# Order of the sums in a seven-product quad: one subtraction and the steps that put the sums together

## The chip, the cores and the metric

The kernel runs on one core of one Trainium2 chip. The metric is the device time of one execution in microseconds (us), lower is better; for the kernel before it is the median of 3 runs.

## What is computed

One decoder layer for 256 tokens of width 2048 in float32: sliding-window attention (16 query heads, 4 key/value heads) and an HGRN2 recurrence side by side, merged by sigmoid gates, then a SwiGLU feed-forward of inner width 5632 and a gated per-layer embedding. Cut to the products that matter here (`w_in` is [2048, 9728], `w_gate_up` is [2048, 11264]):

```python
y = rms_norm(x, g_mix_pre) @ w_in          # q, k, v, the HGRN2 inputs, two gates
...
merged = sigmoid(gate_a) * branch_a + sigmoid(gate_h) * branch_h
x = x + rms_norm(merged @ w_out, g_mix_post)
g, u = split(rms_norm(x, g_ffn_pre) @ w_gate_up)
x = x + rms_norm((silu(g) * u) @ w_down, g_ffn_post)
```

All weight products are made to float32 accuracy on a faster matmul format: each operand is split into a rounded part and the rest, and a product is three matmuls.

## The kernel before

**Weights.** They come from memory in pieces of 2 x 128 rows by 512 columns (`raw`, 512 KB, a DMA of SP). ScalarE (ACT) copies a piece to the rounded part `wh`, VectorE (DVE) subtracts it from the piece and so makes `wl`; both go either as one instruction of 1024 columns for the two row blocks, or as one of 512 for each. TensorE (PE) then runs, for 128 rows, `wh` with `hi`, `wh` with `lo` and `wl` with `hi`, where `hi` and `lo` are the same split of the activations.

**Quads.** Some pieces are taken in twos: two row blocks of two column blocks make a quad b11, b21, b12, b22, and the quad is multiplied with 7 products instead of 8 (a Strassen-Winograd form). `parts_of_quad` makes the seven right sides: b11, b21, b22 and the sums t1 = b11 - b12, t2 = b22 + t1, t4 = b21 - t2, t3 = b22 - b12. `hi(name, src)` is the copy on ACT, `lo(name, src)` the subtraction on DVE, `total(a, b, op)` a sum on DVE into a tile `t`. It is a generator: at each `yield` the planner may put other work between. `by_quads` (L520) runs the matmuls of a quad in the order b11, b21, t1, t2, b22, t4, t3. The left sides of the sums (`sides`, split into `shi` and `slo`) are made by DVE and ACT elsewhere. There are 59 quads: in three pairs of the gate columns of w_in (`gate_pair`), in two columns of w_out, in ten of the eleven blocks of w_gate_up (`swiglu`) and in w_down.

**Banks.** PSUM has eight banks of 128 x 512. While a group of quads runs, four hold the plain products (`cs`) and four the sums (t1, t2, t3, b11). `drop` puts a bank at the end of the queue `banks`; `acc` (for matmuls of weights) and `misc` (for transposes and the like) take the first of the queue. So the order of the drops decides which bank the next work gets and which instruction it waits for.

**Putting together.** After the last quad of a group `put_together` (L567) copies the bank of b11 (p1, ACT) and makes from it and the other three sums the four addends u2, u4, u3 and again u2 (DVE). Then `total` (L585) adds to each of the four `cs` banks its addend and drops the bank. This goes on in 16 groups.

**Order.** Instructions are issued in the order in which the Python program emits them, each engine in its own row. A planner with a rough clock for each engine keeps a heap of generators; `yield A`, `yield V` and `yield T` come back when that engine is estimated to be done with what was issued, `yield 0.3` after that many us. `pump` runs the generators that are due, `hurry` pulls them forward when a bank or a side is lacking. `prefetch_quads` (L443) makes the coming quads' parts a step at a time. So one moved line can shift rows elsewhere.

In `swiglu` the products of gate and up are combined when the four totals are done (`ev_g`, `ev_u`), and `gated` then transposes the result on PE: 4 matmuls `misc<-ident,u` of 128 x 128 for each half of the tokens.

Of the kernel before, what the change touches and what calls it, by code (L numbers as in the profile page):

```python
# [17 lines left out]
ALU = mybir.AluOpType  # L18
# [110 lines left out]
def block_kernel(ctx: ExitStack, tc: tile.TileContext, I, out: bass.AP):  # L129
# [55 lines left out]
    V = InOrder(nc.vector, 0.07, 0.00105)  # L185
# [50 lines left out]
    def slot(s, shape=(P, NB), dt=F32):  # L236
        i = free_slots.popleft()
        t = slots.tile(list(shape), dt, tag=f"s{i}", name=nm(s))
        owner[id(t)] = i, t
        return t  # L240

    def free(*tiles):
        for t in tiles:
            free_slots.append(owner.pop(id(t))[0])

    def room(n):

        while len(free_slots) < n:
            yield 0.3
# [13 lines left out]
    def drop(ps):  # L263
        banks.append(bank_of.pop(id(ps))[0])
# [10 lines left out]
    def act(o, i, f, **kw):  # L275
        return A.activation(o, i, f, **kw)

    def tt(o, a, b, op):
        return V.tensor_tensor(o, a, b, op)
# [84 lines left out]
    def parts_of_quad():  # L364

        w, k, col, raw, _ = loaded.popleft()
        other = loaded.popleft()[3]
        b11, b21, b12, b22 = raw[:, 0, :], raw[:, 1, :], other[:, 0, :], other[:, 1, :]
        parts = {}

        def hi(name, src):
            parts[name] = slot("wh", dt=F32R)
            act(parts[name], src, AF.Copy)

        def total(a, b, op):
            t = slot("t")
            tt(t, a, b, op)
            return t

        def lo(name, src):  # L380
            h, t = parts[name], slot("wl", dt=F32R)
            tt(t, src, h.bitcast(F32), ALU.subtract)
            parts[name] = h, t

        hi("b11", b11)
        hi("b21", b21)
        yield
        t1 = total(b11, b12, ALU.subtract)
        hi("t1", t1)
        lo("b11", b11)  # L390
        yield
        t2 = total(b22, t1, ALU.add)
        hi("t2", t2)
        t4 = total(b21, t2, ALU.subtract)
        hi("t4", t4)
        yield
        lo("b21", b21)
        load_more()
        t3 = total(b22, b12, ALU.subtract)
        hi("b22", b22)  # L400
        yield
        hi("t3", t3)
        lo("t1", t1)
        lo("b22", b22)
        load_more()
        free(t1)
        yield
        lo("t2", t2)
        lo("t4", t4)
        free(t2, t4)  # L410
        yield
        lo("t3", t3)
        free(t3)
        ready.append(((w, k, col), parts, None))

    def load_more():
        if plan:
            load_pair()
# [3 lines left out]
    def begin():  # L422

        if not loaded or len(making) > 1:
            return
        if loaded[0][4]:
            if len(loaded) > 1 and len(free_slots) >= STEP + SPARE:
                making.append(parts_of_quad())
                next(making[-1])
        elif len(in_pool) <= SPLIT or len(free_slots) >= ROOMY:  # L430
            making.append(parts_of_pair())
            next(making[-1])
# [87 lines left out]
    def by_quads(w, n, order, lhs, sides, cs, sums, us, start=True, stop=True, evac=None):  # L520
# [4 lines left out]
        for i, (q, seven) in enumerate(order):  # L525
# [38 lines left out]
            if last:  # L564
                chain(put_together(sums, us))

    def put_together(sums, us):  # L567

        yield T
        yield from room(4)  # L570
        p1, u2, u3, u4 = (slot("u") for _ in range(4))
        act(p1, sums["b11"], AF.Copy)
        drop(sums["b11"])
        yield A
        tt(u2, sums["t2"], p1, ALU.add)
        drop(sums["t2"])
        tt(u4, sums["t1"], u2, ALU.add)
        yield V
        tt(u3, sums["t3"], u2, ALU.add)
        drop(sums["t3"])  # L580
        tt(u2, sums["t1"], u3, ALU.add)
        drop(sums["t1"])
        us.extend([[p1, u3], [u4, u2]])

    def total(us, n, c, ps):  # L585
# [1127 lines left out]
    for at, (pair, gi) in enumerate(DOWN):  # L1713
        if at % 5 == 0:
            ps, us = [[acc(), acc()] for n in range(2)], []
            sums = {"left": len(SEVEN_DOWN[pair])}
# [138 lines left out]
```

## Time and profile before

| what | value |
|---|---|
| median of 3 runs | 1487.96 us (1487.32 to 1491.14) |
| the profiled execution | 1489.56 us |
| its span, from the first to the last recorded instruction | 1487.5 us |
| TensorE clock granted, mean | 0.997 |
| DVE rows `u<-acc,u`, steps and totals together | 132, mean 684 ns |
| DVE rows `t<-raw,t` (t2 and t4) | 118, mean 687 ns |

The profile shows one execution. PE, DVE, ACT and SP are engines; a row like `acc<-wh,hi` names the output's tile and the inputs'. In a timeline row stand the start in us from the begin of the span, the time from start to end, the engine, the operation with its shapes, and a count of equal neighbours that are drawn together; in square brackets the idle time ahead of it and what ended that. An instruction of DVE or of PE may start before its forerunner's end as shown, so the distance of two starts is the measure of what one costs in a row, and PE's ends are modelled. All of the kernel's instructions are recorded in a helper, so all have the line L181; the tiles tell them apart.

### The profile page before, as it was taken

How to read it: one execution, taken by the hardware profiler on the slowest of the kernel's cores; microseconds unless marked ns; L12 is line 12 of the kernel's file. 1: busy time of each engine (PE TensorE's matmuls, PEld its weight loads, DVE VectorE, ACT ScalarE, POOL GpSimd, SP SyncE). 2: the span in 40 equal slices, each digit the busy share in tenths (PEclk: the TensorE clock that was granted, in tenths of full speed). 3: DMA queues.
4: the chain of work that ended last, by engine and by line, in shares of the span. 5: the costliest groups of instructions: out<-in, count | busy, mean ns of one | idle time of the engine just before them, and what ended most of it. 6: DMA issues, size and time to landing. Idle time of an engine off the chain costs nothing.

```text
span 1487.5 us, 19958 instructions
## 1 busy us (share of the span) xinstructions
PE 1469.5 (99%) x6838; PEld 1216.3 (82%) x6838; DVE 1239.9 (83%) x2043; ACT 888.9 (60%) x1417; POOL 62.9 (4%) x107
## 2 busy tenths in 40 slices
PE   9999999999999999999999999999999999999997
PEld 6888888888887888888888888888888887888885
DVE  6878958755999867977899999999988899997773
ACT  7755655566666645665655666565655666575661
POOL 2100000000000100000000000000000000010000
PEclk9999999999999999999999999999999999999998
DMA  9754544345576856866756676576677678797551
GB/s 342 257 188 155 171 141 128 114 128 170 184 240 227 309 185 201 272 227 199 252 182 219 205 238 213 174 230 206 215 239 268 214 252 270 214 336 260 192 188 56
DMA packets 159557, 314.59 MB, mean 211 GB/s; under 512 B 11072, under 2 KB 11520, under 8 KB 159456
## 3 DMA queue, kind: packets, MB, share of 16 engines
q1 hardware_dynamic: 153024, 293.38, 61.0%
q0 software_dynamic: 6256, 19.88, 3.7%
q8 instruction: 53, 0.87, 0.2%
q14 instruction: 48, 0.39, 0.1%
q10 hardware_dynamic: 176, 0.07, 0.0%
HBM read 298.08 MB, written 15.21 MB: 211 GB/s over the span
## 4 chain that ended last, share of the span: by engine, by line
PE 64%; DVE 4%; issue 2%; DMA 1%; ACT 1%; DVEq 0%; POOLq 0%; POOL 0%; ACTq 0%
PE acc L181 63%; DVE wl L181 2%; PE misc L181 1%; DVE u L181 1%; ACT wh L181 1%; DVE t L181 1%; DMA raw<-in_w_in 1%; DMA raw<-in_w_down 0%; DMA raw<-in_w_gate_up 0%; DVE eg L181 0%; DVE slo L181 0%; DVE lo L181 0%; ACT hi L181 0%; DVE sides L181 0%; DVE s L181 0%
## 5 line engine op out<-in xcount | busy, mean ns | idle before, releaser
L181 PE MATMUL acc<-wh,hi 128*128 128x512 f32 x1769 | 700.2, 396 | 3.6 <-DVE u L181 2.4
L181 DVE TENSOR_TENSOR wl<-raw,wh 128x1024 fp32r<-128x1024 f32 (+1 forms) x606 | 595.7, 1007 | 115.4 <-ACT wh L181 113.8
L181 PE MATMUL acc<-wl,hi 128*128 128x512 f32 x1769 | 690.0, 390 | 0.0
L181 PE MATMUL acc<-wh,lo 128*128 128x512 f32 x1769 | 688.9, 389 | 0.0
L181 ACT ACTIVATE wh<-raw 128x1024 fp32r<-128x1024 f32 (+1 forms) x606 | 514.3, 883 | 239.8 <-PE acc L181 101.6
L181 PEld LDWEIGHTS acc<-wl,hi 128*128 128x128 f32 x1769 | 332.0, 188 | 71.2 <-DVE wl L181 1.1
L181 PEld LDWEIGHTS acc<-wh,hi 128*128 128x128 f32 x1769 | 332.3, 188 | 70.6 <-DVE u L181 3.2
L181 PEld LDWEIGHTS acc<-wh,lo 128*128 128x128 f32 x1769 | 332.5, 188 | 66.6 <-issue 0.2
L181 ACT ACTIVATE wh<-t 128x512 fp32r<-128x512 f32 x236 | 145.6, 628 | 106.6 <-DVE t L181 85.9
L181 DVE TENSOR_TENSOR wl<-t,wh 128x512 fp32r<-128x512 f32 x236 | 152.2, 683 | 0.5 <-PE acc L181 0.5
L181 DVE TENSOR_TENSOR u<-acc,u 128x512 f32<-128x512 f32 x132 | 86.3, 684 | 18.8 <-PE acc L181 17.6
L181 PE MATMUL acc<-wh,shi 128*128 128x512 f32 x236 | 91.9, 390 | 1.2 <-ACT shi L181 1.2
L181 PE MATMUL acc<-wh,slo 128*128 128x512 f32 x236 | 91.9, 390 | 0.2 <-DVE slo L181 0.2
L181 PE MATMUL acc<-wl,shi 128*128 128x512 f32 x236 | 91.8, 389 | 0.0
L181 DVE TENSOR_TENSOR t<-raw,t 128x512 f32<-128x512 f32 x118 | 81.1, 687 | 3.7
L181 PEld LDWEIGHTS acc<-wh,shi 128*128 128x128 f32 x236 | 44.3, 188 | 10.8 <-ACT shi L181 1.6
L181 PEld LDWEIGHTS acc<-wh,slo 128*128 128x128 f32 x236 | 44.3, 188 | 9.7 <-DVE slo L181 0.5
L181 PEld LDWEIGHTS acc<-wl,shi 128*128 128x128 f32 x236 | 44.3, 188 | 9.2
L181 POOL DMA_DIRECT2D act<-actd x40 | 21.4, 538 | 601.9 <-DVE wl L181 402.4
L181 DVE TENSOR_TENSOR t<-raw,raw 128x512 f32<-128x512 f32 x59 | 40.3, 684 | 3.9 <-DMA raw<-in_w_gate_up 1.9
L181 DVE TENSOR_TENSOR t<-raw 128x512 f32<-128x512 f32 x59 | 40.3, 684 | 0.0
L181 DVE TENSOR_TENSOR lo<-act,hi 128x512 fp32r<-128x512 f32 x40 | 27.2, 684 | 8.1 <-ACT hi L181 8.0
(214 smaller groups left out, 852.1 us busy)
## 6 DMA issues: line engine op xcount, KB each, us to landing
raw<-in_w_gate_up SPq DMA_DIRECT2D x176, 512.0 KB, 4.6
raw<-in_w_in SPq DMA_DIRECT2D x152, 512.0 KB, 4.3
raw<-in_w_down SPq DMA_DIRECT2D x88, 512.0 KB, 5.5
raw<-in_w_out SPq DMA_DIRECT2D x32, 512.0 KB, 5.5
raw<-in_w_ple_gate SPq DMA_DIRECT2D x32, 512.0 KB, 5.1
act<-actd POOLq DMA_DIRECT2D x40, 256.0 KB, 5.6
raw<-in_w_attn_branch SPq DMA_DIRECT2D x16, 512.0 KB, 5.2
raw<-in_w_hgrn_branch SPq DMA_DIRECT2D x16, 512.0 KB, 5.1
```

The source lines that it names most:

```text
L181: return tc.keep_in_program_order(f(o, *a, **kw))
```

## The change

In the quad, the `wl` of b21 is emitted between t2 and t4, and the generator's pause stands before t4. In `put_together` the second value of u2 is t3 + u4 in place of t1 + u3: both are t1 + t2 + t3 + p1. With it the bank of t1 is dropped after the second step and that of t3 after the last, and the pause by V between u4 and u3 becomes two pauses of 0.5 us.

```diff
--- before.py
+++ after.py
@@ -391,10 +391,10 @@
         yield
         t2 = total(b22, t1, ALU.add)
         hi("t2", t2)
+        lo("b21", b21)
+        yield
         t4 = total(b21, t2, ALU.subtract)
         hi("t4", t4)
-        yield
-        lo("b21", b21)
         load_more()
         t3 = total(b22, b12, ALU.subtract)
         hi("b22", b22)
@@ -574,12 +574,13 @@
         yield A
         tt(u2, sums["t2"], p1, ALU.add)
         drop(sums["t2"])
+        yield 0.5
         tt(u4, sums["t1"], u2, ALU.add)
-        yield V
+        drop(sums["t1"])
         tt(u3, sums["t3"], u2, ALU.add)
+        yield 0.5
+        tt(u2, sums["t3"], u4, ALU.add)
         drop(sums["t3"])
-        tt(u2, sums["t1"], u3, ALU.add)
-        drop(sums["t1"])
         us.extend([[p1, u3], [u4, u2]])
 
     def total(us, n, c, ps):
```

No engine gets other work by it, but two instructions of ACT and two of DVE, where a piece of 1024 columns is done in two of 512. The order changes as follows.

**DVE, from the second pair of gate columns to the third.** The group's steps and totals, before: `acc_3985`, `3984`, `3981`, `3980` are its plain banks, `t_4343`, `t_4360`, `t_4364`, `t_4378` the sums t1, t2, t4, t3 of a quad of the next pair.

```order
L181 TENSOR_TENSOR u_4351<-acc_4032,u_4350 128x512
L181 TENSOR_TENSOR u_4350<-acc_4030,u_4351 128x512
L181 TENSOR_TENSOR wl_4410<-t_4360,wh_4362 128x512
L181 TENSOR_TENSOR wl_4412<-t_4364,wh_4366 128x512
L181 TENSOR_TENSOR wl_4414<-t_4378,wh_4388 128x512
L181 TENSOR_TENSOR wl_4338<-raw_4304,wh_4337 128x1024
L181 TENSOR_TENSOR u_4350<-acc_3985,u_4350 128x512
L181 TENSOR_TENSOR u_4352<-acc_3984,u_4352 128x512
L181 TENSOR_TENSOR u_4351<-acc_3981,u_4351 128x512
L181 TENSOR_TENSOR u_4349<-acc_3980,u_4349 128x512
L181 TENSOR_TENSOR wl_4417<-raw_4322,wh_4416 128x1024
```

The same place in the change; t4 is `t_4372` here. Both extracts begin at the group's u3 and the second u2.

```order
L181 TENSOR_TENSOR u_4351<-acc_4032,u_4350 128x512
L181 TENSOR_TENSOR u_4350<-acc_4032,u_4352 128x512
L181 TENSOR_TENSOR wl_4404<-t_4343,wh_4345 128x512
L181 TENSOR_TENSOR wl_4406<-raw_4280,wh_4380 128x512
L181 TENSOR_TENSOR wl_4410<-t_4360,wh_4362 128x512
L181 TENSOR_TENSOR wl_4412<-t_4372,wh_4374 128x512
L181 TENSOR_TENSOR wl_4414<-t_4378,wh_4402 128x512
L181 TENSOR_TENSOR u_4350<-acc_3985,u_4350 128x512
L181 TENSOR_TENSOR u_4352<-acc_3984,u_4352 128x512
L181 TENSOR_TENSOR u_4351<-acc_3983,u_4351 128x512
L181 TENSOR_TENSOR u_4349<-acc_3982,u_4349 128x512
L181 TENSOR_TENSOR wl_4338<-raw_4304,wh_4337 128x1024
```

The `wl` of t1 and of b22, ahead of the u steps before, now come behind them, and the 1024-column `wl_4338` has gone from before the totals to behind them.

**PE, from one gate_up block to the next** (the one that begins near 812 us in the profile; three more go the same way). Before, the end of the next block's first 12 matmuls (`acc_7731`), the transposes of the two halves of `u`, and the next matmuls:

```order
L181 MATMUL acc_7731<-wh_7580,hi_6507 128x512
L181 MATMUL acc_7731<-wh_7580,lo_6508 128x512
L181 MATMUL acc_7731<-wl_7581,hi_6507 128x512
L181 MATMUL misc_7758<-ident,u_7290 128x128 x4
L181 MATMUL misc_7763<-ident,u_7292 128x128 x4
L181 MATMUL acc_7734<-wh_7589,hi_6377 128x512
L181 MATMUL acc_7734<-wh_7589,lo_6378 128x512
L181 MATMUL acc_7734<-wl_7590,hi_6377 128x512
```

In the change, the end of the old block (`acc_7342`), and what comes after it:

```order
L181 MATMUL acc_7342<-wh_7566,hi_6633 128x512
L181 MATMUL acc_7342<-wh_7566,lo_6634 128x512
L181 MATMUL acc_7342<-wl_7567,hi_6633 128x512
L181 MATMUL misc_7735<-ident,u_7294 128x128 x4
L181 MATMUL acc_7745<-wh_7584,hi_6381 128x512
L181 MATMUL acc_7745<-wh_7584,lo_6382 128x512
L181 MATMUL acc_7745<-wl_7585,hi_6381 128x512
L181 MATMUL misc_7752<-ident,u_7296 128x128 x4
```

Before, the eight transposes stand in a row, behind 12 matmuls of the new block. In the change four stand at its start and four behind its first three matmuls, and the second four go to a bank that is dropped by the second of the four totals (`u<-acc_7341`). On DVE, these totals now follow the u steps at once, where a `wl` of 1024 columns stood between.

**ACT, in w_down, near 1238 us.** `shi_11927` is the rounded left side of the sums for which PE waits; `wh_11922`, `wh_11954` and `wh_11958` are t1, t2 and t4 of a quad. Before, from the copy between t1 and t2 on:

```order
L181 ACTIVATE hi_11937<-act_11848 128x512
L181 ACTIVATE wh_11954<-t_11952 128x512
L181 ACTIVATE wh_11958<-t_11956 128x512
L181 ACTIVATE shi_11927<-sides_11926 128x512
L181 ACTIVATE hi_11968<-act_11849 128x512
L181 ACTIVATE wh_11987<-raw_11864 128x512
L181 ACTIVATE wh_11995<-t_11985 128x512
```

In the change, with `shi_11932`, and t4 in `wh_11986`:

```order
L181 ACTIVATE hi_11945<-act_11862 128x512
L181 ACTIVATE wh_11959<-t_11957 128x512
L181 ACTIVATE shi_11932<-sides_11931 128x512
L181 ACTIVATE hi_11974<-act_11863 128x512
L181 ACTIVATE wh_11986<-t_11984 128x512
L181 ACTIVATE wh_11992<-raw_11857 128x512
L181 ACTIVATE wh_12001<-t_11990 128x512
```

The conversion of t4 has gone from before `shi` to two places behind it.

## The prediction

> **What bounds the kernel now.** I read the page's busy shares and chain first, then TensorE's list of waits, then the timeline at each place where TensorE stops between two matmuls of the quads.
>
> ```profile
> PE 1469.5 (99%) x6838; PEld 1216.3 (82%) x6838; DVE 1239.9 (83%) x2043; ACT 888.9 (60%) x1417; POOL 62.9 (4%) x107
> ...
> PE 64%; DVE 4%; issue 2%; DMA 1%; ACT 1%; DVEq 0%; POOLq 0%; POOL 0%; ACTq 0%
> ```
>
> PE is busy 99% of the span, and of the shares that the chain gives to an engine it has by far the largest. DVE, which does every instruction that this change adds, drops or moves on purpose, is at 83% and mostly off the chain. So time can only be won where PE waits, and lost where PE is made to wait. The list of PE's waits says how much there is to win:
>
> ```profile
> PE acc L181 <- DVE u L181: 2.4, 2, 1.6
> ...
> PE acc L181 <- ACT shi L181: 1.2, 1, 1.2
> ...
> PE misc L181 <- DVE u L181: 0.4, 1, 0.4
> ```
>
> The columns are us in total, times, longest. The rows that have to do with quads are two waits for a `u` (the putting together of sums; 2.4 us), one for `shi` (1.2 us) and a wait of the transposes for a `u` (0.4 us). Even if all went, that is 4.0 us of 1487.96, under 0.3%, which is about what a measurement of this kernel can tell from no change.
>
> **The change part by part.** No instruction is added or dropped in `parts_of_quad` or `put_together`: t1, t2, t4, t3 and the four steps on u2, u4, u3, u2 stay, with the same sizes. What changes is which neighbour stands next to which, when two banks are dropped, and, through the generators' yields, where other work comes between.
>
> *Neighbours on DVE.* There are 59 quads (the first row) and the sums' steps stand in rows like these:
>
> ```profile
> L181 DVE TENSOR_TENSOR t<-raw,raw 128x512 f32<-128x512 f32 x59 | 40.3, 684 | 3.9 <-DMA raw<-in_w_gate_up 1.9
> ```
>
> ```profile
> 415.09 1.48 DVE L181 TENSOR_TENSOR t<-raw,t 128x512 f32<-128x512 f32 x2
> ...
> 463.26 1.88 DVE L181 TENSOR_TENSOR wl<-t,wh 128x512 fp32r<-128x512 f32 x3
> ```
>
> Three `wl` that don't need one another take 1.88 us: with 0.68 for the last, they start 0.60 apart. t2 and t4, where t4 reads t2, take 1.48: t4 starts 0.80 after t2. The change puts `wl` of b21 between them, so a quad saves about 0.2 us of DVE: 59 x 0.2 = 12 us of DVE time. It lies beside PE and is worth nothing by itself where PE has its weights ahead; it counts only before a wait of PE. In `put_together` u3 then u2 was such a pair and now isn't; u2 then u4 stays one, unless something is put between. That is 0.1 us for each of them (four `u` take 2.73 where four totals, which are independent, take 2.47, two bubbles).
>
> [...]
>
> *First gate pair to second.* The fourth total frees the bank for which PE waits:
>
> ```profile
> 426.04 0.50 PE L181 MATMUL acc<-wh,hi 128*128 128x512 f32 x1 [0.78 <-DVE u L181]
> ```
>
> The order of DVE before these totals is unchanged but for t4 and `wl` of b21. Only the bubble of `put_together` is sure, since the u steps here come behind a `wl` that waits for ACT: **-0.1 us** (bounds 0 and -0.3, both bubbles).
>
> *Second gate pair to the third.* Here the order moves.
>
> ```profile
> 458.56 0.68 DVE L181 TENSOR_TENSOR t<-raw 128x512 f32<-128x512 f32 x1
> ...
> 460.61 2.73 DVE L181 TENSOR_TENSOR u<-acc,u 128x512 f32<-128x512 f32 x4
> ...
> 465.06 1.22 DVE L181 TENSOR_TENSOR wl<-raw,wh 128x1024 fp32r<-128x1024 f32 x1
> 466.20 2.47 DVE L181 TENSOR_TENSOR u<-acc,u 128x512 f32<-128x512 f32 x4
> ```
>
> ```profile
> 466.75 0.39 PE L181 MATMUL acc<-wl,hi 128*128 128x512 f32 x1
> 468.73 0.50 PE L181 MATMUL acc<-wh,hi 128*128 128x512 f32 x1 [1.59 <-DVE u L181]
> ```
>
> PE's next matmul is due at 466.75 + 0.23 = 466.98, and the fourth total ends at 466.20 + 2.47 = 468.67; PE starts 0.06 later. In the change the four u steps come straight after t3, and the 1024-column `wl` comes behind the totals. So: t3 starts 0.2 earlier, at 458.37; u steps from 458.97, now 0.71 + 3 x 0.61 = 2.54; five `wl` of 0.60 to 464.5; totals from there, the fourth ended at 464.5 + 2.47 = 467.0. PE would stop for about 0.1 instead of 1.75: **-1.6 us** (bounds -1.1, the moved `wl` alone, 466.20 - 465.06; and -1.75). What is late next is PE itself. What is pushed back, the `wl` of t1 and b22, is wanted only in the quad after this stop, over 5 us later.
>
> *Start of w_down.* PE waits for `shi`, behind two conversions of a `t` on ACT:
>
> ```profile
> 1237.91 1.13 ACT L181 ACTIVATE wh<-t 128x512 fp32r<-128x512 f32 x2
> 1238.95 0.61 ACT L181 ACTIVATE shi<-sides 128x512 fp32r<-128x512 f32 x1
> ...
> 1239.62 0.50 PE L181 MATMUL acc<-wh,shi 128*128 128x512 f32 x1 [1.22 <-ACT shi L181]
> ```
>
> The second of them is t4's and now comes after `shi`. The pair takes 1.04 to the next start, so `shi` and all behind it come 0.52 earlier: **-0.5 us** (bounds 0, and -1.2, the whole wait).
>
> *Transposes in gate_up.* This is the cost. At every second block's end PE transposes earlier results into two `misc` banks. Now 12 matmuls of the next block come first and the eight transposes stand in a row. In the change four stand at the block's start, then three matmuls, then four into a bank that only the *second total* frees, because the totals now follow the u steps at once and their banks stand earlier in the queue of free banks. The place, in four blocks, before the change:
>
> ```profile
> 812.01 0.39 PE L181 MATMUL acc<-wh,hi 128*128 128x512 f32 x1
> ...
> 814.51 0.39 PE L181 MATMUL acc<-wl,hi 128*128 128x512 f32 x1
> ...
> 815.62 0.49 PE L181 MATMUL acc<-wh,hi 128*128 128x512 f32 x1
> ```
>
> ```profile
> 896.25 0.39 PE L181 MATMUL acc<-wh,hi 128*128 128x512 f32 x1
> ...
> 898.75 0.39 PE L181 MATMUL acc<-wl,hi 128*128 128x512 f32 x1
> ...
> 900.56 0.48 PE L181 MATMUL acc<-wh,hi 128*128 128x512 f32 x1
> ```
>
> ```profile
> 981.14 0.39 PE L181 MATMUL acc<-wh,hi 128*128 128x512 f32 x1
> ...
> 983.63 0.39 PE L181 MATMUL acc<-wl,hi 128*128 128x512 f32 x1
> ...
> 985.08 0.48 PE L181 MATMUL acc<-wh,hi 128*128 128x512 f32 x1
> ```
>
> ```profile
> 1065.69 0.39 PE L181 MATMUL acc<-wh,hi 128*128 128x512 f32 x1
> ...
> 1068.18 0.39 PE L181 MATMUL acc<-wl,hi 128*128 128x512 f32 x1
> ...
> 1069.43 0.49 PE L181 MATMUL acc<-wh,hi 128*128 128x512 f32 x1
> ```
>
> ```profile
> 810.10 2.73 DVE L181 TENSOR_TENSOR u<-acc,u 128x512 f32<-128x512 f32 x4
> ...
> 891.48 0.69 DVE L181 TENSOR_TENSOR wl<-raw,wh 128x512 fp32r<-128x512 f32 x1 [0.70 <-ACT wh L181]
> ...
> 895.03 2.73 DVE L181 TENSOR_TENSOR u<-acc,u 128x512 f32<-128x512 f32 x4
> ```
>
> ```profile
> 979.55 2.73 DVE L181 TENSOR_TENSOR u<-acc,u 128x512 f32<-128x512 f32 x4
> ```
>
> ```profile
> 1063.91 2.73 DVE L181 TENSOR_TENSOR u<-acc,u 128x512 f32<-128x512 f32 x4
> ```
>
> The first row of each PE fence is the block's first matmul, the second the last before the transposes, the third the first behind them. Matmuls stand (898.75 - 896.25) / 11 = 0.227 apart. At 814.51 nothing waits: 815.62 - 814.51 = 1.11, less 0.23, is 0.88 for eight, 0.11 each. The other three take 1.81, 1.45 and 1.25, so PE waits there now for 0.70, 0.34 and 0.14, in all 1.18 us.
>
> After the change PE comes to the second four 4 x 0.11 + 3 x 0.227 = 1.12 after the block's start: 813.13, 897.37, 982.26, 1066.81. The bank is free when the second total ends: u steps 0.71 + 0.61 + 0.61 and, as the first total now reads what the step just ahead of it wrote, 0.71; then 0.60 and 0.68, 3.91 after the first u step, and 0.06 until PE runs, 3.97. The first u step starts as before, but 0.2 earlier in the first block, where DVE runs through; in the others DVE stops for ACT behind t3 (0.70 at 891.48), which eats that gain. So the bank is there at 813.88, 899.00, 983.52, 1067.88: waits of 0.75, 1.63, 1.26, 1.07, in all 4.71. Less the 1.18 of today: **+3.5 us** (bounds: -1.2, all waits gone, and +8.1, each block's u steps later by one 1024-column conversion, 4 x 1.14 more).
>
> *Other blocks.* The eight transposes that stand at the other four blocks' ends move forward into the middle of those blocks, behind totals that end long before: nothing. At the last gate_up block they come earlier and close behind their data: **+0.1 us** (0 to 0.4, the wait of transposes in the list).
>
> **The sum** is -0.1 - 1.6 - 0.5 + 3.5 + 0.1 = **+1.4 us**. The profiled execution took 1489.56 us (span 1487.5 and 2.06 around it); it would take 1491.0. It lies 1.6 above the median of the three runs, 1487.96 (1487.32 to 1491.14), so the median goes to **1489.4**, 0.1% more: no change by measurement, for two gains of which the moved transposes take back more than both.
>
> **The rivals.**
>
> *The gains land, and the transposes cost nothing new.* If DVE reaches the totals some 0.9 us earlier in each block, the new waits are as long as today's. The bubbles that go could do it, a few quads of 0.2 in a block; against it stands the wait for ACT at 891.48, which takes up what DVE wins ahead of it. -0.1 - 1.6 - 0.5 = -2.2: 1485.8; with today's 1.18 gone too, 1484.6.
>
> *Slower: the transposes wait for a later total.* In the change t4 comes one `wl` later, and ACT converts t4, b22 and t3 in that order behind it. If that order pushes the u steps in the four blocks back by as much as one conversion of 1024 columns (1.14 us, 465.06 to 466.20), each wait grows by it: +1.4 + 4 x 1.14 = +6.0, 1494.0. It decides from a new wait of 1.6 us a block, net of today's (6.6 in all). For it: DVE does wait for ACT there already. Against: at those places ACT has work of its own ahead of t4's conversion, under which 0.4 us more of DVE hides.
>
> *Nothing shows.* The half-step yields pull the steps apart in few places, the u steps stay in a row, and PE's stops go on as they are, since the planner's estimates fill what is freed: 0 +- 0.5, 1488.0. Against it: the second gate pair's order does move.
>
> **How the numbers follow.** Forecast 0.52, gains without cost 0.19, nothing 0.15, slower 0.12, and 0.02 for something that I don't see. The range 1485.4 to 1492.8 holds the forecast with its bounds on the first three terms and a part of the fourth, all of "nothing" and most of "gains"; left out are the slower rival and the end with today's waits gone. Faster by over 0.3% means under 1483.5, which needs more than all waits of PE in the list around quads: 0.03. Slower by over 0.3% means above 1492.4: the slower rival and an edge of the forecast, 0.13. Within: 0.84.
>
> **What would show it.** After, PE's wait near 468.7 us shrinks to 0.1 or so and the one near 426 stays; the wait for `shi` falls to about 0.7; `misc` waits for `u` four times, once in each of the blocks beginning near 812, 896, 981 and 1066, 0.8 to 1.6 us each; t and `wl` alternate on DVE with starts 0.60 apart. No `misc` waits, or `misc` waits beyond 2 us, would make it wrong; so would a wait of PE in a place that has none today.

## The result, and the profile after

The changed kernel takes 1494.46 us (median of 5 runs, 1494.15 to 1494.57), the kernel before, measured beside it, 1487.96. The ratio is 1.0036, with a 95% interval of 1.0025 to 1.0048: slower by 0.36%, 5.4 us by the ratio and 6.5 by the medians. Forecast were 1489.4, a change too small to measure, and a range up to 1492.8: wrong, the loss is several times larger than the +1.4 us of the sum. In the experiments below, one execution at a granted clock of 0.75 took 1843 us and is left out of the times and ratios.

The page of the profiled execution (1494.15 us, span 1492.4) has the same busy times to within 0.7% on PE, DVE and ACT. The chain gives PE 92%, where it gave 64% before. That isn't the change: three more profiles of the same changed kernel (below) have 68%, 66% and 92%.

```profile
PE 1471.3 (99%) x6838; PEld 1216.4 (82%) x6838; DVE 1239.0 (83%) x2045; ACT 883.0 (59%) x1419; POOL 62.9 (4%) x107
...
PE 92%; DVE 2%; DMA 2%; issue 2%; ACT 1%; SPq 0%; DVEq 0%; POOLq 0%; POOL 0%; ACTq 0%
```

PE's list of waits (us in total, times, longest) shows where the time is:

```profile
PE acc L181 <- ACT actT L181: 3.2, 4, 0.8
PE misc L181 <- DVE u L181: 2.0, 4, 0.7
...
PE acc L181 <- DVE lo L181: 1.2, 2, 0.9
...
PE acc L181 <- DVE u L181: 1.0, 1, 1.0
```

The second row is the forecast's cost, four waits of the transposes. The first was not forecast at all: four waits of weight matmuls (`acc`) for `actT`, the copy of a transposed tile by ScalarE (ACT). The timeline of PE in the middle of a gate_up block shows one:

```profile
823.36 0.39 PE L181 MATMUL acc<-wl,hi 128*128 128x512 f32 x1
823.59 1.03 PE L181 MATMUL misc<-ident,u 128*128 128x128 f32 x8
825.42 0.50 PE L181 MATMUL acc<-wh,hi 128*128 128x512 f32 x1 [0.80 <-ACT actT L181]
```

And ACT at the same place:

```profile
824.28 1.08 ACT L181 ACTIVATE actT<-misc 128x512 f32<-128x512 f32 x2 [4.94 <-PE misc L181]
```

Eight transposes, then 0.80 us idle, until ACT has copied both banks that the transposes filled (824.28 + 1.08 = 825.36). The next matmul is the first product of the block's first quad, b11. Its bank is one of these two. The reason stands in `by_quads`: the banks of the sums are taken in the order t1, t2, t3, b11, and used in the order b11, t1, t2, t3. Four banks are free there; the transposes take the first two of the queue and put them back at its end, t1, t2 and t3 take the others and one of those, and b11, which is needed first, gets the bank dropped last. The fourth experiment tests this.

The other places of the forecast follow. At the start of a block the transposes wait as foretold, for less:

```profile
812.87 0.66 PE L181 MATMUL misc<-ident,u 128*128 128x128 f32 x4 [0.26 <-DVE u L181]
...
899.00 0.66 PE L181 MATMUL misc<-ident,u 128*128 128x128 f32 x4 [0.74 <-DVE u L181]
```

From the second gate pair to the third the stop has nearly gone, from 1.98 us between two starts to 0.39:

```profile
467.66 0.39 PE L181 MATMUL acc<-wl,hi 128*128 128x512 f32 x1
468.05 0.50 PE L181 MATMUL acc<-wh,hi 128*128 128x512 f32 x1
```

And DVE in the same stretch has the order and the pitch that were foretold:

```profile
457.45 0.69 DVE L181 TENSOR_TENSOR t<-raw,t 128x512 f32<-128x512 f32 x1
458.05 0.69 DVE L181 TENSOR_TENSOR wl<-raw,wh 128x512 fp32r<-128x512 f32 x1
458.65 0.69 DVE L181 TENSOR_TENSOR t<-raw,t 128x512 f32<-128x512 f32 x1
```

t2 and t4 are 1.20 us apart with a `wl` between them; before, t4 came 0.80 behind t2, and the `wl` took 0.60 elsewhere. So 0.2 us of DVE are won in a quad, as forecast. What went wrong is where PE's transposes went.

### The profile page after: what moved, and what is told of

It is laid out like the page before. It is cut to its first block, busy times and chain, and to the rows that moved or that the text cites. A ratio compares the mean times of both kernels' runs of the same rounds, so it can differ in the third digit from the quotient of the medians.

```text
span 1492.4 us, 19961 instructions
## 1 busy us (share of the span) xinstructions
PE 1471.3 (99%) x6838; PEld 1216.4 (82%) x6838; DVE 1239.0 (83%) x2045; ACT 883.0 (59%) x1419; POOL 62.9 (4%) x107
## 4 chain that ended last, share of the span: by engine, by line
PE 92%; DVE 2%; DMA 2%; issue 2%; ACT 1%; SPq 0%; DVEq 0%; POOLq 0%; POOL 0%; ACTq 0%
PE acc L181 87%; PE misc L181 6%; DMA raw<-in_w_in 1%; DVE wl L181 1%; DVE u L181 1%; DMA raw<-in_w_ple_proj 1%; ACT wh L181 1%; DMA raw<-in_w_gate_up 0%; ACT actT L181 0%; DVE t L181 0%; SPq L181 0%; DVE eg L181 0%; ACT hi L181 0%; DVE s L181 0%; DVE lo L181 0%
```

## The experiments

Two theories stood against one another: **M**, that the loss lies in the middle of the blocks, in the bank that b11 is given; and **R**, the forecast's own, that it lies in the transposes at the blocks' starts. Times are medians; ratios are to the kernel before, measured on the same chip in the same series (1488.26 us for the first four, 1488.77 for the next four).

**Only the quad's part.** From the kernel before:

```diff
         t2 = total(b22, t1, ALU.add)
         hi("t2", t2)
+        lo("b21", b21)
+        yield
         t4 = total(b21, t2, ALU.subtract)
         hi("t4", t4)
-        yield
-        lo("b21", b21)
```

> Only the quad's part of the change: wl of b21 between t2 and t4, the pause ahead of t4; put_together as before. Of the transposes only those in the middle of a gate_up block move, as in the change; those at the block's start stay as before. Theory M (the cost is in the middle: the sum of b11 takes the bank in which transposes have just been, and PE waits about 1.04 us for ScalarE's copy, in four blocks): about +4 us over before, some 1492 us, with four waits of acc for actT near 0.8 us each. Theory R (the cost is the transposes at the block's start, that wait for the second total): no such waits here, so the time of before within 1 us, about 1488.

Measured: 1490.7 us, ratio 1.0013 (1.0004 to 1.0022). The four waits are there, and no wait of `misc` for `u`:

```profile
PE acc L181 <- ACT actT L181: 3.2, 4, 0.8
...
PE acc L181 <- DVE lo L181: 1.1, 2, 0.8
PE acc L181 <- DVE u L181: 1.0, 2, 0.5
```

Slower without the waits that R speaks of, so R alone is not the cause. It is less than M's 4 us, in part because this kernel also has gains: its waits for `u` are 1.0 us where they were 2.4.

**Only the sums' part**, with the quad as before:

```diff
         drop(sums["t2"])
+        yield 0.5
         tt(u4, sums["t1"], u2, ALU.add)
-        yield V
+        drop(sums["t1"])
         tt(u3, sums["t3"], u2, ALU.add)
+        yield 0.5
+        tt(u2, sums["t3"], u4, ALU.add)
         drop(sums["t3"])
-        tt(u2, sums["t1"], u3, ALU.add)
-        drop(sums["t1"])
```

> Only the steps that put the sums together: reordered, with two pauses of 0.5 us; the quad as before. Transposes move at the block's start and in its middle, both as in the change. M: four waits for actT of 0.8 us, and with the waits of misc for u some 5 to 6 us over before, 1493 to 1494 us. R: the waits of misc for u alone, 1 to 3.5 us over before, 1489 to 1491.5. If the t2-t4 bubbles in the quad matter as much as the rest, it is slower than the whole change.

Measured: 1497.25 us, ratio 1.0054 (1.0042 to 1.0067). The median is above that of the whole change, but the two intervals overlap, and the five executions run from 1494.64 to 1499.45. It has both kinds of waits, and in its profile one that neither theory has:

```profile
PE acc L181 <- ACT shi L181: 3.6, 1, 3.6
PE acc L181 <- ACT actT L181: 3.5, 4, 1.1
PE misc L181 <- DVE u L181: 1.6, 4, 0.7
```

The wait for `shi` is at the start of w_down; the first two matmuls behind it start 0.81 us apart, where it is 0.34 behind the wait at 825.42 in the change (last section). In this profile ACT stood idle for 5.96 us until a weight piece of w_down had come from memory; it copied that piece at 1243.58 us and reached `shi`, four rows behind, at 1246.10. So either part by itself moves transposes into the middle of the blocks; the sums' part moves those at the starts too.

**The whole change, with both pauses by VectorE's clock** (from the changed kernel):

```diff
         drop(sums["t2"])
-        yield 0.5
+        yield V
         tt(u4, sums["t1"], u2, ALU.add)
...
         tt(u3, sums["t3"], u2, ALU.add)
-        yield 0.5
+        yield V
         tt(u2, sums["t3"], u4, ALU.add)
```

> The whole change, but with both pauses of put_together by the planner's clock of VectorE instead of 0.5 us. The transposes then go behind 12 or more matmuls at the blocks' ends, as before the change, and none stand ahead of the sum of b11 in the middle. M: no wait for actT, so about 4 us under the change, and 1.6 us under before for the second pair's gain that stays: 1486 to 1488 us. R: 1 to 3.5 us under the change.

Measured: 1487.46 us, ratio 0.9991 (0.9983 to 1.0). Both kinds of waits are gone, and the reordered sums are all there; by the ratios some 6.5 us of the change hang on two pauses:

```profile
PE acc L181 <- DVE u L181: 1.6, 1, 1.6
PE warm L181 <- DVE junk L181: 1.4, 1, 1.4
PE misc L181 <- DMA x<-in_x: 0.9, 1, 0.9
PE acc L181 <- DVE lo L181: 0.3, 1, 0.3
```

This removes M's and R's cause together and so doesn't tell them apart; the next run does.

**The changed kernel with b11's bank taken first.** The order of instructions is that of the change on every engine; only the banks differ:

```diff
-                sums.update({k: acc() for k in ("t1", "t2", "t3", "b11")})
+                sums.update({k: acc() for k in ("b11", "t1", "t2", "t3")})
```

> The whole change with the same order of instructions on every engine; only the banks of the four sums are taken in the order b11, t1, t2, t3 instead of t1, t2, t3, b11, so that the product that comes first gets the bank that has been free for longest. M: the four waits for actT go (4.2 us), and the one wait of 1.0 us for u near 427 us: about 5 us under the change, 1489 to 1490 us. R: the banks of the sums have no part in it, so the time of the change, 1494.5.

Measured: 1491.43 us, ratio 1.0014 (1.0005 to 1.0023). The transposes stand where they stood, and PE no longer stops behind them:

```profile
821.43 1.03 PE L181 MATMUL misc<-ident,u 128*128 128x128 f32 x8
822.22 0.48 PE L181 MATMUL acc<-wh,hi 128*128 128x512 f32 x1
```

From the first transpose to the next matmul it is 0.79 us, where the change took 825.42 - 823.59 = 1.83: a stop of 1.04 us, four times, 4.2 us. That is M's cause, shown. But where M expected about 5 us back, some 3 came. The list of waits says why:

```profile
PE misc L181 <- DVE u L181: 4.6, 4, 1.9
...
PE acc L181 <- DVE lo L181: 1.2, 2, 0.9
```

The waits at the blocks' starts have grown from 2.0 to 4.6 us. What PE waits for there is a `u` of DVE. In the change PE came to that place 1.04 us later for the stop in the block before, and so waited that much less. The distances fit: from the first of the four waiting transposes to the last it is 258.0 to 258.5 us in the four profiles of the change (the other three stand below), and 257.4 in the second profile of this kernel. Three stops, 3.1 us, were taken out between them, and at most 1.1 was won. So R's cost is real too, and it is larger without M's.

**The change again**, beside the others:

> The changed kernel again, beside the others on one chip. Its first profile and that of before differ by 4.9 us of span, their medians by 6.5. M (the waits seen in the trace are all): 5 to 6.5 us over before. If part of the 6.5 is a chip's or a run's own, less; a wait that ends in a stretch of matmuls at half pace would show as starts 0.43 us apart behind it.

Measured: 1494.94 us, ratio 1.0035 (1.0025 to 1.0045), so the loss is not one series' own. Its profile has the waits of the first, 3.2 us for `actT` and 2.3 for `u` by `misc`, and no stretch of half pace.

**All of the arithmetic, no pause moved** (from the kernel before):

```diff
         t2 = total(b22, t1, ALU.add)
         hi("t2", t2)
+        lo("b21", b21)
         t4 = total(b21, t2, ALU.subtract)
         hi("t4", t4)
         yield
-        lo("b21", b21)
...
         yield V
         tt(u3, sums["t3"], u2, ALU.add)
+        tt(u2, sums["t3"], u4, ALU.add)
         drop(sums["t3"])
-        tt(u2, sums["t1"], u3, ALU.add)
         drop(sums["t1"])
```

> All of the change's arithmetic and neighbours (wl of b21 between t2 and t4; u2, u4, u3, then u2 from t3 and u4), but every pause where it was before the change, and the banks dropped in the order t3, t1. The transposes stay at the blocks' ends. M: no waits for actT or new ones for u, so no slower than before: within 1.5 us of it, below rather than above (bubbles of DVE worth 0.3 us, the waits near 426 and 468 us at most 2.7). A theory by which the reordered sums themselves cost time: some us over before.

Measured: 1487.92 us, ratio 0.9994 (0.9985 to 1.0003): no difference, and no wait for `actT`, as M says. The other half of the expectation was wrong. The transposes stand where they stood before, or three matmuls later, and yet four of them wait for `u`:

```profile
PE misc L181 <- DVE u L181: 1.8, 4, 0.5
```

In the first profile of before it was 0.4, once. Against that, the wait near 468 us is 0.16 where it was 1.59. So the reordered sums move waits about, and in all they neither cost nor bring anything that can be measured.

**The kernel before with b11's bank first** (the edit of the fourth experiment):

> The kernel before, with the sums' banks taken in the order b11, t1, t2, t3 and nothing else. M (the product that comes first waits for the bank freed last): the waits for u near 426 us (0.9) and 468 us (1.75) go, 2.7 us under before, about 1485.5; the transposes' waits at the blocks' ends may take back up to 1 us. R: no difference.

Measured: 1487.32 us (ten executions), ratio 0.9986 (0.9976 to 0.9995), 2 us by the ratio. The wait near 426 us is gone, the next one not:

```profile
PE acc L181 <- DVE u L181: 1.2, 1, 1.2
```

PE now waits for the first of the four totals, not for the last. In the profile of before the first total of the second turn ended at 466.88, and PE was due at 466.98. Here PE is due 0.8 us earlier, for the stop that is gone at the first turn, and the first total ends at 467.46; PE starts at 467.52 where it started at 468.73. So the two turns together win 1.2 us, and not the 2.7 of the expectation, which added two waits that stand behind the same engine.

**The pauses by VectorE's clock and b11's bank first**, both edits on the changed kernel:

> The change with both pauses by VectorE's clock and the banks in the order b11, t1, t2, t3. M: what the profile of the pauses' kernel won (3.5 us) and its last wait for u of 1.6 us near 427 us: about 5 us under before, 1482.5 to 1484, the fastest so far. If DVE is what is late at each turn, less: 3 to 4 us under before.

Measured: 1485.15 us, ratio 0.9969 (0.9956 to 0.9981): the lowest median of all, 4.6 us under before by the ratio. All that is left of the waits around quads is the last row, 0.2 us (the first two rows are waits near the start, ahead of the quads):

```profile
PE warm L181 <- DVE junk L181: 1.4, 1, 1.4
PE acc L181 <- DVE lo L181: 0.3, 1, 0.3
PE misc L181 <- DVE u L181: 0.2, 1, 0.2
```

**Four more profiles, one execution each**: before, the change twice, and the change with b11's bank first. Beside them one more execution of before took 1491.29 us. They were to settle why the medians differ by 6.2 to 6.5 us, and the first two profiles by only 4.9 of span.

> The kernel before, one more profile. Its first profiled execution took 1489.56 us, 1.6 above its median. If that execution had a wait of its own, the sum of PE's waits in quads here is 1.5 us smaller and the span some 1486; if single executions only scatter, the same waits within 0.5 us each.

Measured: 1486.38 us, span 1484.3 where the first had 1487.5. The wait for `shi` at the start of w_down isn't there:

```profile
PE acc L181 <- DVE u L181: 2.0, 2, 1.4
...
PE acc L181 <- DVE lo L181: 0.3, 1, 0.3
PE acc L181 <- ACT wh L181: 0.2, 1, 0.2
```

> The changed kernel, a third profile. Its medians lie 6.2 to 6.5 us over before, its two profiles 4.1 and 4.9 us of span. M with half pace: in some executions a wait grows past 1.6 us and the matmuls behind it start 0.43 us apart, 2 us more; then such a stretch shows here or in the next run. Otherwise spans of 1491.5 to 1493 without one.

> As the run before it: the changed kernel once more, to see whether waits near the start of w_down (1239 to 1265 us) or at the blocks' starts differ between executions by 1 us or more.

Measured: 1493.56 and 1493.75 us, spans 1491.8 and 1492.0, with 3.2 us for `actT` in both, 2.9 and 2.7 for `u` by `misc`, and no half pace. Four profiles of the change have spans of 1491.6 to 1492.4, mean 1492.0; the two of before 1487.5 and 1484.3, mean 1485.9. Single executions of before scatter more than the 1.3 us between 4.9 and 6.2: here it took 1486.38 and 1491.29, and its two profiled executions lie on either side of its median of 1487.96. So the difference of two single profiles is no measure of the loss; the medians are.

> The change with b11's bank first, one more profile. In its first, the transposes near 982 us waited 1.9 us and the next 8 matmuls started 0.43 us apart instead of 0.23. If a wait of some 1.9 us is what sets the half pace, it comes again with a wait that long and not without.

Measured: 1491.68 us. The wait near 983 us was 2.17, longer than the 1.93 of the first time, and the matmuls behind it started 0.23 us apart. The length of the wait alone does not set the half pace.

## Why the prediction was wrong

By its steps, in its order:

- **What bounds the kernel** (PE, with at most 4.0 us to win): not contradicted. The best version wins 4.6 us by the ratio, with an interval of 2.8 to 6.5.
- **Neighbours on DVE**: right, as the pitch of 0.60 shows.
- **First gate pair to second, -0.1**: not contradicted, and too small to be seen. PE idles 0.42 to 0.95 us there in the four profiles of the change, 0.78 and 0.62 in the two of before.
- **Second gate pair to the third, -1.6**: right. The stop shrank by 1.59 (1.98 to 0.39 between starts); against the second profile of before it is 1.35 (1.74 to 0.39).
- **Start of w_down, -0.5**: wrong in what it took for granted. One wait of one execution was priced. With the same order of rows on every engine the wait for `shi` was 1.22 us in the first profile of before, none in the second, and 0.63 in the kernel before with b11's bank first. In the first profile ACT had waited 5.04 us for weights from memory just ahead of it. In its place the change has a wait for `lo` near 1265 us, 0.5 to 0.9 in its four profiles, and none there in the two of before. In the change DVE makes that `lo` behind two `wl` that stood after it before.
- **Transposes in gate_up, +3.5**: the mechanism was right, the size not. New waits of 4.71 us were worked out. The lists say 2.0, 2.3, 2.9 and 2.7 of idle time; counted from start to start, as the forecast counted, it is 2.7 to 3.5. The working took PE's arrival from the old trace; in fact PE came later, for the stop in the middle of the block before. Where that stop was taken away, the waits are 5.2 and 5.3 counted the same way. The 1.18 us set against them were again one execution's: the second profile of before has 0.15 by the same count.
- **Other blocks: "behind totals that end long before: nothing"**: this is the step that failed. 4 x 1.04 = +4.2 us. It asked only when the transposes' own data and bank are ready, and they were. It did not ask who gets the bank *after* them: the next product in PE's order was given the bank that they had just filled, and PE waited for the copy that empties it, 1.04 us each time (the rows at 823.59, 824.28 and 825.42). The prediction itself had named such a wait, in a place that had none, as a sign that it is wrong. At the last block, where it had +0.1, the traces show 0.05 to 0.07 against the second profile of before.

The sum with measured sizes can be taken from the traces, since the weight matmuls run in the same order in all kernels: the start of the same matmul is compared in two traces. Against the second profile of before, the four profiles of the change have on average nothing at the first turn, -1.3 at the second, +3.2 at the blocks' starts, +4.3 in their middle and +1.1 near 1265 us: +7.3, where the spans differ by 7.7. That profile lies below the median of before. Against its first profile, which was itself 1.4 us longer at the blocks' starts and 1.8 at the start of w_down, the spans differ by 4.5. The medians, 6.2 to 6.5 apart, lie between.

The rival that came near the result in time (1494.0, transposes that wait for a later total) is not what happened: its waits at the blocks' starts should have been 1.14 us longer each than the forecast's, and they were shorter. That its time fits is luck. The rival "gains without new cost" is what the experiment with VectorE's pauses is, though its gain is smaller: 1487.46, 1.3 us by the ratio where the rival had 2.2.

## What to carry to other kernels

Where a pool hands out banks in the order in which they come free, moving a small user (eight transposes) changes which bank every later user gets; ask of each moved instruction not only what it waits for, but who gets its buffer next, and how soon. Take buffers in the order in which they will be used: that one line was worth 2 us to the kernel before and 3 to the changed one, by the ratios. And stalls in series behind one late engine didn't add up here: with b11's bank first, 1.2 us were won of 2.7 in the kernel before, and some 3 of 4.2 in the changed one. Each that was removed was partly paid at the next, so a gain or a loss is to be worked out from the engine that is late, with the other's arrival as it will be, not as it was. Last, a wait of one profiled execution is a sample: a term that is priced from it wants a second profile.

## What was not expected of the hardware

After two of the long waits of PE its matmuls ran at about half pace. In the first profile of the change with b11's bank first:

```profile
982.43 0.67 PE L181 MATMUL misc<-ident,u 128*128 128x128 f32 x4 [1.93 <-DVE u L181]
...
983.33 0.63 PE L181 MATMUL acc<-wh,lo 128*128 128x512 f32 x1
983.75 0.63 PE L181 MATMUL acc<-wl,hi 128*128 128x512 f32 x1
...
986.57 0.40 PE L181 MATMUL acc<-wh,hi 128*128 128x512 f32 x1
986.81 0.40 PE L181 MATMUL acc<-wh,lo 128*128 128x512 f32 x1
```

Starts are on average 0.43 us apart instead of 0.24, for eight matmuls: about 1.5 us more. The trace has the granted clock beside it: 0.50 from 982.95 to 986.36 us, and 1.00 around it. In the sums' kernel it is 0.50 behind the wait of 3.60, from 1246.33 to 1253.16. The mean granted clock of these two executions is 0.996 and 0.995; in the twelve other profiles it is 0.997 or 0.998. The clock stayed at 1.00 behind the wait of 1.59 (before), and behind the one of 2.17 (the second profile with b11's bank first) the matmuls kept their pace of 0.23 to 0.24.

What halves the clock is not shown. It came with waits of 1.93 and 3.60 us and not with 1.59 and 2.17, so the length of the wait alone does not decide it.
